# Token-major RWKV values for two groups at once, with put-off side steps and a longer recursion

## The chip, the cores and the metric

The kernel runs on one core of one Trainium2 chip. The metric is the device time of one execution in microseconds (us); lower is better. The engines are named as in the profile: PE is TensorE (PEld its weight loads), DVE is VectorE, ACT is ScalarE, POOL is GpSimd, SP is SyncE, which here only issues transfers.

## What is computed

One transformer block over 256 tokens of width 2048, in fp32: a normalised input is multiplied by one wide matrix `w_in`, three branches work on pieces of the product (attention, an RWKV-7 time mix, attention to a memory), and gated projections bring them back together. The change touches the RWKV branch:

```
proj = rms_norm(x, g) @ w_in                      # r_b, k_b, v_b, z_b: 1536 columns each
def token_shift_lerp(p, mu):
    prev = pad(p by one token)[:, :-1]
    return p + (prev - p) * mu                    # for r, k and v
# per head, over the tokens t:
sa    = state @ a_t
state = state * w_t + sa * b_t + v_t * k_t
y_t   = state @ r_t
# then a norm per head, plus sum(r*k*r_k) * v, times silu(z)
```

The scan is not run token by token. The kernel works on chunks of 128 tokens and solves a triangular system for each head and chunk.

## The kernel before

**Rounds.** The program is one list of jobs, each a slice of a weight matrix (`Job`). A job of 256 columns has four chunks of 512 KB and computes feature-major ("fm"): the weight slice is the stationary operand, the tokens stream, and for each of 16 row blocks and each half there is a matmul over 512 columns (L308) and one over 256 (L309), because each operand is split into a high and a low part. A "wide" job has 512 columns in eight chunks; there the tokens are stationary and three matmuls of 512 columns (L306) stand for each row block and half. One chunk is one round: 16 matmuls (8 pairs) of an fm job or 12 of a wide one. For each chunk SP issues one transfer (`issue_dma`, L259), ACT makes the high part (L270) and DVE the low part (L273). At most three chunks are loaded and three more split ahead.

**Side steps.** All else is written as Python generators ("lanes"). After each round `step_lanes` runs each lane that is due by one step, up to its next `yield`; `yield n` means n rounds of rest. `force` runs lanes with no round between. What a lane issues stands in every engine's queue right behind that round. Side results of PE go to the PSUM tile `psd`, of which there are four (`ps_side`); the rounds have four others (`pm`).

**RWKV.** Six groups of four heads (256 columns) each have jobs R, K, V and Z. `rkv_evac` and `shift_lerp` take a job's result: ACT copies two pieces per half, POOL adds (L323), POOL subtracts the shifted row (L435), DVE finishes (L431). `pairs_lane` makes decays (L521, L527, scans at L539) and the operands `AR` and `BK`; then, in one step, it transposes two arrays for head sums (L590) and V and BK to token-major `tok` (L599 to L601, read by ACT at L602 and DVE at L604). `rw_lane` makes Gram matrices (L622; DVE reads them at L626 and L627 with four `psd` tiles per chunk), inverts them in a recursion over 31 columns on DVE (L674, L678) that rests at each fourth column, joins blocks (L700 to L732), applies the inverse (L641, L743, L751 to L765), transposes back (L780), normalises, and transposes again (L817). `attn_a` is the attention of one group: scores L838 and L840, a softmax that ends with a scaling on ACT (L861), transposes L868, values L876 and L878, whose `psd` tile is read by L881 once `zsa` is there.

## Time and profile before

| what | value |
|---|---|
| median of 3 runs | 1479.6 us (1477.62 to 1480.51) |
| the profiled execution | 1478.29 us |
| its span, first to last instruction | 1476.5 us |
| PE busy | 1449.2 us, 98% of the span |
| DVE busy | 946.2 us, 64% |
| ACT busy | 747.3 us, 51% |
| POOL busy | 181.8 us, 12% |
| mean granted PE clock | 0.997 |

Busy time counts a matmul from its start to its modelled end, and matmuls overlap, so what one costs is read from start to start. Idle time of an engine stands in brackets behind the instruction that ended it. The RWKV and attention lanes lie in the first 735 us or so; afterwards come the memory branch and the projections.

### The profile page before, as it was taken

The page shows a single profiled execution, that of the slowest core. Times are in us where ns is not written, and L with a number is a line of the kernel's source. Part 1 is how long each engine was busy: PE and PEld are TensorE (multiplying, and loading weights), DVE is VectorE, ACT ScalarE, POOL GpSimd, SP SyncE. Part 2 cuts the span into 40 slices and gives each one's busy share as a digit, 9 for nine tenths or more (in the row PEclk, how much of TensorE's full clock was granted, in tenths as well). Part 3 has the DMA queues.
Part 4 walks back from the last instruction along what each step waited for, and adds up shares of the span by engine and source line. Part 5 has one row for each costly group of instructions (what it writes and reads, how often), then busy time and mean ns, then how long its engine had stood idle before and what let it go on. Part 6 is the DMA issues. An engine that isn't in the chain of part 4 may idle for free.

```text
span 1476.5 us, 22151 instructions
## 1 busy us (share of the span) xinstructions
PE 1449.2 (98%) x8315; PEld 1222.3 (83%) x8315; DVE 946.2 (64%) x1855; ACT 747.3 (51%) x1122; POOL 181.8 (12%) x252
## 2 busy tenths in 40 slices
PE   7999999999999999999999999999999999999997
PEld 6887888888888788788888888888888888888887
DVE  5778697796795786784666555655545545545555
ACT  5546546466456456445666454643443444444443
POOL 4312202212212222211100000000000000000011
PEclk9999999999999999999999999999999999999999
DMA  5665555456465465465575555566556556555753
GB/s 180 192 179 163 159 147 169 143 167 173 133 184 151 134 172 159 135 178 158 162 221 187 172 169 174 167 196 192 187 188 195 188 187 194 188 188 192 262 200 130
DMA packets 207968, 258.88 MB, mean 175 GB/s; under 512 B 28172, under 2 KB 146596, under 8 KB 207220
## 3 DMA queue, kind: packets, MB, share of 16 engines
q1 hardware_dynamic: 201872, 247.11, 54.5%
q10 hardware_dynamic: 4164, 6.71, 1.3%
q0 software_dynamic: 1824, 3.65, 0.8%
q8 instruction: 65, 1.06, 0.3%
q14 instruction: 43, 0.35, 0.1%
HBM read 253.74 MB, written 6.05 MB: 176 GB/s over the span
## 4 chain that ended last, share of the span: by engine, by line
PE 89%; DVE 4%; DMA 2%; ACT 1%; issue 1%; POOL 1%; SPq 0%; ACTq 0%; DVEq 0%
PE pm L306 43%; PE pm L308 24%; PE pm L309 12%; PE psd L622 2%; DVE wt L273 1%; DMA raw<-in_w_in_dram 1%; DVE fs_t L674 1%; PE psd L641 1%; PE psd L1037 1%; PE psd L743 1%; DMA NB<-d 1%; PE psd L154 1%; DMA x_sb<-in_x_dram 1%; ACT wt L270 1%; DVE X L678 1%
## 5 line engine op out<-in xcount | busy, mean ns | idle before, releaser
L273 DVE TENSOR_TENSOR wt<-raw,wt 128x1024 fp32r<-128x1024 f32 (+1 forms) x451 | 559.1, 1242 | 437.4 <-ACT wt L270 433.8
L270 ACT ACTIVATE wt<-raw 128x1024 fp32r<-128x1024 f32 (+1 forms) x452 | 477.2, 1057 | 494.0 <-PE pm L306 256.5
L308 PE MATMUL pm<-hT,wt 128*128 128x512 f32 (+1 forms) x1632 | 587.1, 402 | 0.0
L309 PE MATMUL pm<-hT,wt 128*128 128x256 f32 (+1 forms) x1632 | 458.5, 281 | 3.5 <-DVE wt L273 3.4
L308 PEld LDWEIGHTS pm<-hT,wt 128*128 128x128 f32 (+1 forms) x1632 | 305.7, 187 | 76.3 <-issue 4.2
L306 PE MATMUL pm<-wt,hT 128*128 128x512 f32 x1440 | 335.4, 391 | 0.0
L306 PEld LDWEIGHTS pm<-wt,hT 128*128 128x128 f32 x1440 | 268.6, 188 | 57.6 <-issue 1.7
L309 PEld LDWEIGHTS pm<-hT,wt 128*128 128x128 f32 (+1 forms) x1632 | 307.5, 188 | 6.2 <-DVE wt L273 6.0
L306 PE MATMUL pm<-wt,mg 128*128 128x512 f32 (+1 forms) x384 | 79.3, 367 | 0.0
L306 PEld LDWEIGHTS pm<-wt,mg 128*128 128x128 f32 x384 | 65.7, 189 | 12.5
L1183 POOL MEMSET sso<- 128x16 f32 x1 | 0.1, 117 | 607.0 <-PE pm L306 607.0
L674 DVE TENSOR_TENSOR fs_t<-X,NB 128x30 f32<-128x30 f32 (+13 forms) x354 | 64.9, 223 | 7.5 <-DMA NB<-d 7.1
L306 PE MATMUL pm<-wt,yas 128*128 128x512 f32 x288 | 67.6, 395 | 0.0
L306 PE MATMUL pm<-wt,ybs 128*128 128x512 f32 x288 | 67.6, 395 | 0.0
L323 POOL TENSOR_TENSOR lraw<-lraw,et 128x256 f32<-128x256 f32 (+1 forms) x38 | 45.1, 1207 | 167.2 <-ACT lraw L322 167.2
L306 PEld LDWEIGHTS pm<-wt,ybs 128*128 128x128 f32 x288 | 54.3, 188 | 12.6
L306 PEld LDWEIGHTS pm<-wt,yas 128*128 128x128 f32 x288 | 54.3, 188 | 12.7
L317 ACT ACTIVATE et<-pm 128x256 f32<-128x256 f32 (+1 forms) x112 | 42.6, 382 | 40.3 <-PE pm L309 37.6
L678 DVE TENSOR_TENSOR X<-X,fs_t 128x30 f32<-128x30 f32 (+13 forms) x354 | 56.3, 194 | 0.6
L306 PE MATMUL pm<-wt,mT 128*128 128x512 f32 x192 | 45.8, 395 | 0.0
L308 PE MATMUL pm<-mT,wt 128*128 128x512 f32 x128 | 45.4, 395 | 0.0
L306 PE MATMUL pm<-wt,ycs 128*128 128x512 f32 x192 | 45.3, 395 | 0.0
(299 smaller groups left out, 1324.3 us busy)
## 6 DMA issues: line engine op xcount, KB each, us to landing
raw<-in_w_in_dram SPq DMA_DIRECT2D x320, 512.0 KB, 3.7
raw<-in_w_mem_kv_dram SPq DMA_DIRECT2D x32, 512.0 KB, 3.5
raw<-in_w_out_dram SPq DMA_DIRECT2D x32, 512.0 KB, 4.4
raw<-in_w_proj_a_dram SPq DMA_DIRECT2D x24, 512.0 KB, 4.2
raw<-in_w_proj_b_dram SPq DMA_DIRECT2D x24, 512.0 KB
raw<-in_w_proj_c_dram SPq DMA_DIRECT2D x16, 512.0 KB, 4.4
NB<-d SPq DMA_DIRECT2D x24, 128.0 KB, 3.4
fr<-fd ACTq DMA_DIRECT2D x6, 385.0 KB
```

What stands on the lines that cost most here:

```text
L154: pe.transpose(pv[:, a, t], src[:, t, (k + a) * 128:(k + a + 1) * 128], ident)
L270: act.activation(w[:, :, 0], r, AF.Copy)
L273: eng.tensor_tensor(w[:, :, 1], r, w[:, :, 0].bitcast(FT), OP.subtract)
L306: pe.matmul(ps[:, 0:j.n], l, r, start=first and n == 0, stop=last and n == 2)
L308: pe.matmul(ps[0:j.m], hi, both, start=first, stop=last, skip_group_check=True)
L309: pe.matmul(ps[0:j.m, 256:512], lo, top, start=False, stop=last, skip_group_check=True)
L317: act.activation(t, ps[0:j.m, 256:512], AF.Copy)
L323: pool.tensor_tensor(j.dst[f], j.dst[f], t, OP.add)
L622: pe.matmul(pv[h][:, w].rearrange("p x t -> p (x t)"), BK[rows, q, c, w * 128:(w + 1) * 128], AR[rows, q, c].rearrange("p x t -> p (x t)") ...
L641: pe.matmul(pv[:, 2 * q + h], GS[:, c * 4 + 2 * q + h, 2], tok[:, q, c, rows], start=(c == 0), stop=True, skip_group_check=True)
L674: dve.tensor_tensor(t, X[:, k0:8, c:c + 1].to_broadcast([128, m, hi - lo]), NB[:, lo:hi, c].rearrange("p (o n) -> p o n", o=1).to_broadcas ...
L678: dve.tensor_tensor(X[:, k0:8, lo:hi], X[:, k0:8, lo:hi], t, OP.add)
```

## The change

Group V of two neighbouring groups becomes one wide job, so V comes token-major (`vt`) from PE, and needs no transposes. The shift by one token is now a shift across partitions: two transfers on SP copy `vt` to `vsh` one row down, POOL subtracts and multiplies by `mu_v` (which it loads as a row broadcast to 128 partitions), DVE adds (L507 of the new program). `tok` keeps only the two transposes of BK, in one `psd` tile. The Grams' readers of `tok` read `vt` instead. A lane may yield a pair: `(d, more)` rests d rounds, and then for up to `more` rounds goes on only if another lane has taken a `psd` tile in that round. `pairs_lane` no longer waits for V, and from the second group on it makes its transposes once the group before has finished its first half. The recursion rests at each third column. Jobs stand in another order. In the new program the recursion's L674 is L719, and the low part of the weights, L273, is L288.

```diff
+    used = [0]
     def ps_side():
+        used[0] += 1
         return psum.tile([128, 512], FT, name="psd", bufs=4)
...
     def step_lanes():
         clock[0] += 1
+        n = used[0]
+        due = [ln for ln in lanes if ln[0] <= clock[0]]
+        for ln in due:
+            if not ln[2]:
+                step(ln)
+        for ln in due:
+            if ln[2] and ln[0] <= clock[0]:
+                if used[0] != n or clock[0] >= ln[0] + ln[2]:
+                    ln[2] = 0
+                    step(ln)
...
+    def v_evac(g):
+        def f(ps, t):
+            if t == 0:
+                if g:
+                    force(("rw", g - 2))
+                for i in range(2):
+                    St["v", g + i] = E["rw"].tile([128, 2, 256], FT, name="vt", bufs=3)
+            for i in range(2):
+                act.activation(St["v", g + i][:, t], two(ps)[:, i], AF.Copy)
+            if t == 1:
+                add_lane(v_lane(g), 2)
+        return f
+    def v_lane(g0):
+        for g in (g0, g0 + 1):
+            vt = St["v", g]
+            sh = E["rw"].tile([128, 2, 256], FT, name="vsh")
+            mu = E["rw"].tile([128, 1, 256], FT, name="muv")
+            pool.memset(sh[0:1, 0], 0.0)
+            pool.dma_start(mu[:, 0], bass.AP(tensor=mu_v.tensor, offset=mu_v.offset + g * 256, ap=[[0, 128], [1, 256]]))
+            nc.sync.dma_start(sh[1:128], vt[0:127])
+            nc.sync.dma_start(sh[0:1, 1], vt[127:128, 0])
+            yield 3
+            pool.tensor_tensor(sh, sh, vt, OP.subtract)
+            pool.tensor_tensor(sh, sh, mu.to_broadcast([128, 2, 256]), OP.mult)
+            yield 2
+            dve.tensor_tensor(vt, vt, sh, OP.add)
+            flags["V", g] = True
+            yield 1
...
-        yield 3
+        yield (3, 2) if g else 3
...
-        yield from wait(("V", g))
-        yield 1
+        if g:
+            yield from wait(("half_free", g - 1))
...
-        v = St.pop(("V", g))
+        tok = rw.tile([128, 2, 2, 128], FT, name="tok")
+        p = ps_side()
+        pv = p.rearrange("p (a q c) -> p a q c", a=2, q=2)
+        for a in range(2):
+            for q in range(2):
+                pe.transpose(pv[:, a, q], BK[:, q, 0, 128 * (1 - a):128 * (2 - a)], ident)
+        act.activation(tok[:, :, 0], pv[:, 0], AF.Copy)
         for q in range(2):
-            p = ps_side()
-            pv = p.rearrange("p (a c) -> p a c", a=4)
-            for c in range(2):
-                pe.transpose(pv[:, c], v[:, q, c * 128:(c + 1) * 128], ident)
-            pe.transpose(pv[:, 2], BK[:, q, 0, 128:256], ident)
-            pe.transpose(pv[:, 3], BK[:, q, 0, 0:128], ident)
-            act.activation(tok[:, q, 0:3], pv[:, 0:3], AF.Copy)
...
-            if c % 4 == 0:
+            if c % 3 == 0 and c < 31:
                 yield 1
...
-        yield 3
+        yield (2, 2)
         pT = rw.tile([128, 2, 384], FT, name="pT")
...
-               Job(w_in2, VB + c, 256, 16, hT, rkv_evac(g, "V", "muv"), add=pool),
...
+    BJ = [Job(w_in2, VB + 512 * i, 512, 16, hT, v_evac(2 * i), mode="wide") for i in range(3)]
+    for g, (a0_, a1_) in enumerate(((0, 2), (2, 5), (5, 7), (7, 10), (10, 12), (12, 16))):
+        jobs += RJ[3 * g:3 * g + 2] + BJ[g // 2:g // 2 + 1 - g % 2] + AJ[a0_:a1_] + RJ[3 * g + 2:3 * g + 3 - (g == NG - 1)]
```

PE, the transposes of the second group. Before they share a round with the back transposes L780 of the group before and use five `psd` tiles:

```order
L306 MATMUL pm_1861<-wt_1807,hT_74 128x512 x6
L780 MATMUL psd_1919<-ident_85,YT_1707 128x128 x4
L590 MATMUL psd_1928<-ident_85,sg_1765 128x128 x4
L590 MATMUL psd_1934<-ident_85,R_1456 128x128 x4
L599 MATMUL psd_1942<-ident_85,V_1821 128x128 x2
L600 MATMUL psd_1942<-ident_85,BK_1845 128x128
L601 MATMUL psd_1942<-ident_85,BK_1845 128x128
L599 MATMUL psd_1950<-ident_85,V_1821 128x128 x2
L600 MATMUL psd_1950<-ident_85,BK_1845 128x128
L601 MATMUL psd_1950<-ident_85,BK_1845 128x128
```

Afterwards the same place on PE (L635 was L590, L645 was L600 and L601, L790 was L743, the product with the inverse):

```order
L321 MATMUL pm_1809<-wt_1667,hT_74 128x512 x6
L790 MATMUL psd_1816<-W_1784,XF_354 128x64 x4
L635 MATMUL psd_1822<-ident_85,sg_1702 128x128 x4
L635 MATMUL psd_1828<-ident_85,R_1403 128x128 x4
L645 MATMUL psd_1837<-ident_85,BK_1793 128x128 x4
L321 MATMUL pm_1802<-wt_1709,hT_74 128x512 x6
```

The transposes of V are gone, the others have moved up by three rounds to another neighbour, and the round uses four tiles. Next on PE, the first Gram chunk of that group, before in a round of its own:

```order
L306 MATMUL pm_1861<-wt_1849,hT_74 128x512 x6
L622 MATMUL psd_1977<-AR_1767,BK_1845 128x256
L622 MATMUL psd_1978<-AR_1767,BK_1845 128x256
L622 MATMUL psd_1977<-AR_1767,BK_1845 128x256
L622 MATMUL psd_1978<-AR_1767,BK_1845 128x256
L622 MATMUL psd_1987<-AR_1767,BK_1845 128x256
L622 MATMUL psd_1988<-AR_1767,BK_1845 128x256
```

Afterwards (L667 was L622, L812 was L765, the end of the second half of the group before):

```order
L810 MATMUL psd_1863<-GS_353,vt_835 64x128
L812 MATMUL psd_1863<-GS_353,W_1784 64x128
L667 MATMUL psd_1876<-AR_1704,BK_1793 128x256
L667 MATMUL psd_1877<-AR_1704,BK_1793 128x256
L667 MATMUL psd_1876<-AR_1704,BK_1793 128x256
L667 MATMUL psd_1877<-AR_1704,BK_1793 128x256
L667 MATMUL psd_1886<-AR_1704,BK_1793 128x256
L667 MATMUL psd_1887<-AR_1704,BK_1793 128x256
```

The Gram chunk has joined the round that ends the group before, and with that round's own tile it asks for five of the four. SP, from the Gram transfers of a group to those of its inverse, before:

```order
L259 DMA raw<-in_w_in_dram 128x2x512 x8
L259 DMA raw<-in_w_in_dram 128x4x256 x4
L652 DMA d_2057<-GS 32x8x32 x4
L259 DMA raw<-in_w_in_dram 128x4x256
L663 DMA NB<-d_2057 32x1024 x4
L259 DMA raw<-in_w_in_dram 128x4x256 x9
```

And afterwards (L697 was L652, L708 was L663, L274 is the weight transfer):

```order
L697 DMA d_3012<-GS 32x8x32 x4
L274 DMA raw<-in_w_in_dram 128x4x256
L708 DMA NB<-d_3012 32x1024 x4
L501 DMA vsh<-vt 127x512
L502 DMA vsh<-vt 1x16x16
L274 DMA raw<-in_w_in_dram 128x4x256 x6
L501 DMA vsh<-vt 127x512
L502 DMA vsh<-vt 1x16x16
L274 DMA raw<-in_w_in_dram 128x4x256 x6
```

The shifted copies of V stand between weight transfers, in the rounds of the recursion.

## Rows read from the trace of the kernel before

**Rows 1.** Stretch of the lanes: PE, PEld, DVE, ACT, POOL busy (instructions), clock, DMA share, GB/s.

```profile
100.00:700.00 600.00, 591.65 (x4080) 504.07 (x4079) 447.36 (x1259) 329.96 (x576) 127.75 (x178) 1.00 0.55 158
```

**Rows 2.** Waits of PE: us in total, times, longest.

```profile
PE pm L309 <- DVE wt L273: 3.4, 5, 0.9
PE psd L599 <- DVE Y L790: 3.4, 5, 0.9
```

**Rows 3.** Timeline of PE: start, us, what; fm pairs, then a wide job.

```profile
299.69 0.40 PE L308 MATMUL pm<-hT,wt 128*128 128x512 f32 x1
...
314.88 0.40 PE L308 MATMUL pm<-hT,wt 128*128 128x512 f32 x1
...
934.58 21.97 PE L306 MATMUL pm<-wt,hT 128*128 128x512 f32 x96
956.39 16.91 PE L306 MATMUL pm<-wt,yas 128*128 128x512 f32 x72
```

**Rows 4.** Timeline of PE: four transposes between rounds.

```profile
315.24 0.60 PE L817 MATMUL psd<-ident,Y 128*128 128x128 f32 x4
315.60 0.48 PE L308 MATMUL pm<-hT,wt 128*128 128x512 f32 x1
```

**Rows 5.** Timeline of PE: the transposes of groups 2 and 4, counted from 0.

```profile
284.25 0.60 PE L780 MATMUL psd<-ident,YT 128*128 128x128 f32 x4
...
287.04 0.48 PE L308 MATMUL pm<-hT,wt 128*128 128x512 f32 x1
...
492.74 0.60 PE L780 MATMUL psd<-ident,YT 128*128 128x128 f32 x4
...
495.15 0.41 PE L599 MATMUL psd<-ident,V 128*128 128x128 f32 x2 [0.93 <-DVE Y L790]
...
496.07 0.48 PE L308 MATMUL pm<-hT,wt 128*128 128x512 f32 x1
```

**Rows 6.** Timeline of PE: a Gram chunk of groups 0, 3 and 4.

```profile
80.42 2.78 PE L622 MATMUL psd<-AR,BK 64*128 64x256 f32 x16
...
394.57 2.00 PE L622 MATMUL psd<-AR,BK 64*128 64x256 f32 x16
...
499.02 1.56 PE L622 MATMUL psd<-AR,BK 64*128 64x256 f32 x10
501.15 1.10 PE L622 MATMUL psd<-AR,BK 64*128 64x256 f32 x6 [0.57 <-DVE GS L627]
```

**Rows 7.** Timeline of PE, then DVE: one attention tile, written and read.

```profile
426.96 0.38 PE L878 MATMUL psd<-pT,va 128*128 128x128 f32 x2
...
513.70 0.68 DVE L881 TENSOR_TENSOR ya<-psd,zsa 128x512 f32<-128x512 f32 x1
```

**Rows 8.** A stretch of group 0's recursion, columns as in the first group.

```profile
114.70:130.50 15.80, 13.55 (x73) 10.58 (x71) 14.35 (x72) 9.81 (x18) 2.66 (x5) 1.00 0.50 145
```

**Rows 9.** Timelines of DVE and of ACT in that stretch.

```profile
115.01 0.36 DVE L674 TENSOR_TENSOR fs_t<-X,NB 128x40 f32<-128x40 f32 x2
...
118.17 0.35 DVE L674 TENSOR_TENSOR fs_t<-X,NB 128x40 f32<-128x40 f32 x2
...
126.44 1.40 DVE L674 TENSOR_TENSOR fs_t<-X,NB 128x28 f32<-128x28 f32 x2
...
117.24 1.50 ACT L861 ACTIVATE as<-as,asm 128x256 f32<-128x256 f32 x4 [2.55 <-DVE asm L857]
...
120.58 2.94 ACT L270 ACTIVATE wt<-raw 128x1024 fp32r<-128x1024 f32 x3
```

**Rows 10.** Waits of DVE: us in total, times, longest.

```profile
DVE V L431 <- POOL et L435: 6.3, 6, 1.7
```

**Rows 11.** Groups by form: xcount | busy us, mean ns | idle before.

```profile
L273 DVE TENSOR_TENSOR wt<-raw,wt 128x1024 fp32r<-128x1024 f32 x448 | 556.3, 1244 | 437.4 <-ACT wt L270 433.8 <-PE pm L306 3.1
L435 POOL TENSOR_TENSOR et<-lraw 128x512 f32<-128x512 f32 x18 | 24.2, 1344 | 1.4
```

More of the change, by code (lines that the diff above doesn't have):

```diff
@@ L201, in add_lane @@
     def add_lane(gen, rest=0):
-        lanes.append([clock[0] + rest, gen])
+        lanes.append([clock[0] + rest, gen, 0])
     def later(rest, fn, *a):
@@ L208, in later, with step @@
         add_lane(g(), rest)
+    def step(ln):
+        try:
+            d = next(ln[1])
+            d, more = d if isinstance(d, tuple) else (d or 1, 0)
+            ln[0], ln[2] = clock[0] + d, more
+        except StopIteration:
+            lanes.remove(ln)
     def step_lanes():
         clock[0] += 1
-        for ln in list(lanes):
-            if ln[0] > clock[0]:
-                continue
-            try:
-                d = next(ln[1])
-                ln[0] = clock[0] + (d or 1)
-            except StopIteration:
-                lanes.remove(ln)
+        n = used[0]
[8 more added lines that the diff above has]
+                    step(ln)
     def force(*keys):
@@ L559, in pairs_lane @@
         AR = rw.tile([128, 2, 2, 2, 128], FT, name="AR", bufs=2)
-        tok = rw.tile([128, 2, 4, 128], FT, name="tok", bufs=2)
         nb = rw.tile([128, 2, 2, 2], FT, name="nb", bufs=2)
@@ L593, in pairs_lane @@
         dve.reciprocal(nb, nb)
[L594 to L605 removed]
+        tok = rw.tile([128, 2, 2, 128], FT, name="tok")
[5 more added lines that the diff above has]
+        act.activation(tok[:, :, 0], pv[:, 0], AF.Copy)
+        for q in range(2):
+            dve.tensor_tensor(tok[:, q, 1].rearrange("p (h v) -> p h v", h=2), pv[:, 1, q].rearrange("p (h v) -> p h v", h=2),
+                              nb[:, 0, q].rearrange("p (h o) -> p h o", o=1).to_broadcast([128, 2, 64]), OP.mult)
         flags["rkv_free", g] = True
@@ L612, in rw_lane @@
         S = E["S"]
+        vt = None
         halves = [slice(64 * h, 64 * h + 64) for h in range(2)]
@@ L640, in from_v @@
                 for h, rows in enumerate(halves):
-                    pe.matmul(pv[:, 2 * q + h], GS[:, c * 4 + 2 * q + h, 2], tok[:, q, c, rows], start=(c == 0), stop=True,
+                    pe.matmul(pv[:, 2 * q + h], GS[:, c * 4 + 2 * q + h, 2], vt[:, c, 128 * q + 64 * h:128 * q + 64 * h + 64], start=(c == 0), stop=True,
                               skip_group_check=True)
@@ L705, in rw_lane @@
             act.activation(X64[s, :, s], XN[s], AF.Copy)
+        yield from wait(("V", g))
+        vt = St["v", g]
         W = from_v(0)
@@ L750, in rw_lane @@
                     for h, rows in enumerate(halves):
-                        pe.matmul(pv[rows, q], tok[:, q, 2, rows], tok[:, q, 0, rows], start=True, stop=False)
-                        pe.matmul(pv[rows, q], tok[:, q, 3, rows], W[:, 1, q * 2 + h], start=False, stop=True)
+                        pe.matmul(pv[rows, q], tok[:, q, 0, rows], vt[:, 0, 128 * q + 64 * h:128 * q + 64 * h + 64], start=True, stop=False)
+                        pe.matmul(pv[rows, q], tok[:, q, 1, rows], W[:, 1, q * 2 + h], start=False, stop=True)
                 for rows in halves:
@@ L762, in rw_lane @@
                     u = c * 4 + 2 * q + h
-                    pe.matmul(pv[rows, q], tok[:, q, c, rows], GS[:, u, 3], start=(c == 0), stop=False,
+                    pe.matmul(pv[rows, q], vt[:, c, 128 * q + 64 * h:128 * q + 64 * h + 64], GS[:, u, 3], start=(c == 0), stop=False,
                               skip_group_check=True)
@@ L806, in rw_lane @@
                 Yq[:, c * 4:c * 4 + 4].rearrange("p (q h) v -> p q h v", q=2),
-                tok[:, :, c].rearrange("p q (h v) -> p q h v", h=2),
+                vt[:, c].rearrange("p (q h v) -> p q h v", q=2, h=2),
                 bs[:, c].rearrange("p q (h o) -> p q h o", o=1).to_broadcast([128, 2, 2, 64]), OP.mult)
@@ L812, in rw_lane @@
         yield from wait(("zsb", g))
+        yield (1, 2)
         p = ps_side()
```

9 lines of the change are left out of this document (2 added, 7 removed).

## The prediction

> **What bounds the kernel now.** I read the busy times by stretch first. Between 100 and 700 us, where the lanes run, PE is busy 591.65 of 600 us at a granted clock of 1.00, while DVE is busy 447.36, ACT 329.96 and POOL 127.75 [rows 1]. So TensorE is the bound; the time falls only if its queue gets shorter or one of its gaps closes. The waits of PE came second: what it waits for in the rounds is the split weights from DVE, 3.4 us in five waits, and in the transposes step a `psd` tile, 3.4 us in five waits, given free by a DVE operation of another lane [rows 2]. These are waits on the one late instruction; what the engine loses around them is larger, so I went through its timeline, from the start of one matmul to the start of the next.
>
> Three prices come from it. An fm pair (512 and 256 columns) takes 0.353 us: 43 pairs lie between 299.69 and 314.88. A wide job's matmul takes 0.227 us: 96 from 934.58 to 956.39 [rows 3]. Four transposes between two rounds hold the next main matmul back by 0.36 us, and that one takes 0.48 instead of the usual 0.40: 0.44 in all, 0.11 us for each instruction [rows 3, 4]. So a full-array side step pays for its instructions, and next to nothing for the interruption itself.
>
> **The change part by part.** *V as a wide job.* For two groups 2 x 4 chunks x 8 pairs = 64 pairs x 0.353 = 22.6 us become 8 chunks x 12 = 96 matmuls x 0.227 = 21.8: 0.8 us less, three times, -2.4 us, all on the path.
>
> Here a rule can be weighed against the trace. The trace has 0.353 us for 768 columns and 0.227 for 512 [rows 3]: per column the pair costs 4% more. The Trainium skill, TensorE: Matmul & The Clock Gate, section "Wait — 56ns, not 53.3ns?", gives a start to start of the columns at 2.4 GHz plus some 2.5 ns for each matmul. By that, as an estimate, a pair takes 0.325 us and a wide matmul 0.216, the three wide jobs save only 0.3 us, and the sum below comes out 2.1 us higher. The trace does not agree with it for either kind, so the sum goes by the rows.
>
> *Transposes.* 24 of V go (4 for each of six groups): 24 x 0.11 = -2.6 us. BK's stay. Both kinds of matmul that read `tok` keep their number and form.
>
> *Tiles in the transposes step.* Before, this step and the back transposes next to it take five tiles of four, 20 transposes. In group 2 they take 2.79 us, 284.25 to 287.04; in group 4 3.33, 492.74 to 496.07, with 0.93 of waiting [rows 5]. At 0.11 each, less what the last restart holds (counted above), 20 are 2.1 to 2.2. The excess in my walk through all six is 0.24 (group 0), about 0.68 (1 to 3) and 1.21 (4, 5): 4.7 us. Afterwards the round has four tiles (one of L790, two of L635, one of L645), so no tile has to come back within it. I take -4.7. Bounds: 0, if a tile is still held from the round before, to -4.7.
>
> *Grams.* A Gram chunk takes 2.00 us of PE in group 3, but 2.78 in group 0 and 3.23 (499.02 to 502.25) in group 4, where PE waits for DVE to empty the third pair [rows 6]. The reason in groups 4 and 5: an attention value tile is written at 426.96 and read only at 513.70, once `zsa` is there [rows 7], so three tiles are left for four. Four chunks x 1.23 + 0.78 = 5.7 us. The new job order makes that holding shorter: by the built program's order it falls on both chunks of group 4 and none of group 5, and group 0's chunk stays as it is. Left: 2 x 1.23 + 0.78 = 3.2, so -2.5. Bounds: 0 (group 5 is met too) to -5.7 (none is).
>
> *Put-off steps.* Interruptions of PE fall from 123 to 114. For full-array steps I cost a join at nothing, by the 0.11 that already holds the restart [rows 4]. A Gram chunk uses half of the rows (its form is 64 x 256 [rows 6]), and such steps show about 0.1 us more on entering or leaving; five of them now follow the likewise tiled end of the previous group's second half: -0.5. Against it: that round then asks for five tiles of four. The fourth Gram tile waits until ACT has copied the round's own first tile, while PE has the rest of that tile's and three Gram tiles' work before it, some 1 us; I take 0, and as the upper bound +1.23 a time, as where group 4 lacks a tile [rows 6]: +6.2 for five. Put-off steps (L868, L876, L817) issue no transfer of their own, so no queue is moved past. The Gram transfers come with their chunk, some three rounds earlier on SP; the `wd` and `wa` loads on POOL stay ahead of their lane's first rest.
>
> *Rests at three columns.* In group 0's recursion PE is busy 13.55 of 15.80 us and DVE 14.35 [rows 8]. One rest of four columns with its split takes 3.16 us (115.01 to 118.17) on DVE, and an fm round takes 8 x 0.353 = 2.83 on PE: DVE loses 0.3 us a round until the split weights run out. With the split at 1.24 [rows 11], a column is 0.48, and three with a split 2.7 us, under 2.83. A second cause stands beside it: ACT's L861 waits 2.55 us for a DVE operation behind the columns, and the splits on ACT start only at 120.58 [rows 9]. I take the gap of this stretch, 15.80 - 13.55 = -2.3 us; bounds 0 and -3.4, all of PE's waits for split weights [rows 2]. The later groups' recursions show little of it. Their longer recursion (two or three rounds more) delays only what follows in its lane, which is not last on PE.
>
> *New work.* The V lane puts two operations a group on POOL, six groups (twelve, some 1.34 us each by L435 [rows 11]), as V did before in three; their sum falls. They now stand in recursion rounds. DVE's add of V waits for POOL; behind it on DVE stand the splits, and behind those PE. Such a wait existed before: V's L431 waited for POOL 6 times, 6.3 us, the longest 1.7 [rows 10], and the chunks split ahead (three, 8.5 us of PE) hid it. On SP the copies of V wait for ACT's `vt` and POOL's memset, and weight transfers stand behind them; three loaded and three split chunks, 17 us, cover that. I take +1.0 for all this, with 0 to +18 (below), nearer to 0 because of that cover. A gain below 0 I exclude: it is added work, and DVE and POOL were not the bound.
>
> **Sum.** -2.4 - 2.6 - 4.7 - 2.5 - 0.5 - 2.3 + 1.0 = -14.0. The profiled execution has a span of 1476.5 and a time of 1478.29, so 1.8 lies outside; the median is 1.3 above it. 1476.5 - 14.0 + 1.8 = 1464.3, and + 1.3 = **1465.6 us**.
>
> **The rivals.**
> *Tile waits take the place of those removed.* The five joined Gram rounds have one tile too few. Each then costs what group 4's chunk costs, 1.23 [rows 6]: +6.2, 1471.8. For it: the tiles are exactly one short. Against: PE has about 1 us to do before the fourth, and only one ACT copy is needed.
>
> *The joins save more.* If rejoining side steps also spares the restart gaps that I put at zero, nine interruptions at 0.11 and the remaining Gram excess (3.2) go too: 1465.6 - 1.0 - 3.2 = 1461.4. Against it: the four-transpose step shows no such price [rows 4].
>
> *DVE and POOL hold each other up in the recursion.* One pair of L674 took 1.40 us at 126.44 where its like took 0.35 at 118.17 [rows 9]: 1.05 us lost while POOL was at work. Twelve POOL operations of V now stand there: 12.6 us on DVE. DVE has a quarter of its time free [rows 1], so I give half of it to PE, 6.3, and the gap of 2.3 stays: 1465.6 + 8.6 = 1474.2. If all of it reaches PE, 1480.5, no change. For it: POOL's work on V is moved to just where DVE was 91% busy [rows 8]. The Trainium skill, SBUF — State Buffer, section "Who interferes with whom", says that a DVE instruction with two SBUF inputs and a POOL instruction that reads SBUF exclude each other; L674 is such a one, and the row agrees.
>
> *Slower: the adds of V park DVE.* Each add (six) finds POOL still at its first operation and waits the longest wait seen plus one more operation, 1.7 + 1.34 = 3.0 us [rows 10, 11], and all reaches PE, since three columns and a split leave only 0.1 us a round to win the lead back: 6 x 3.0 = +18, 1483.6. It decides once the waits of one recursion together use up the three split chunks (8.5 us); with two V lanes in a row that takes other delays besides. Against it: the lane rests two rounds, 5.6 us, between POOL's operations (2.7) and the add.
>
> **How the numbers follow.** The measurement tells about 0.2%, 3 us, from no change. Chances: the forecast 0.52 (1465.6), tile waits 0.20 (1471.8), joins save more 0.08 (1461.4), half of the collisions 0.08 (1474.2), all of them 0.06 (1480.5, same), parked DVE 0.06 (1483.6, slower). Faster by over 0.2% is 0.52 + 0.20 + 0.08 + 0.08 = 0.88, within it 0.06, slower 0.06. The range must hold 0.8: from 1459, the larger gain with a little of the bounds of the Grams and the rests, to 1474, the tile waits with 2 us of unplanned gaps; the collisions and the parking are left out above.
>
> **What would show it.** In the profile after: the wide V jobs at 0.227 us a matmul; PE's count lower by 120; no wait of L635 or L645 for a tile; sixteen transposes in 1.8 us; the five joined Gram chunks (L667 behind L812) at 2.0 us, or at 3.2 if the first rival is right; PE's waits for split weights in group 0's recursion gone; L719 pairs of over 1 us few. Waits of DVE's L507 for POOL of over 3 us, followed by waits of PE for L288, would show the slower case. What would make the prediction wrong is a price for moved steps that the trace of before does not have: the same lanes now meet other neighbours in nearly every round, and a step that was covered may end last.

## The result: slower, by transfers that the sum had not priced

The changed kernel takes 1521.18 us (median of 4 runs, 1519.83 to 1523.54) against 1478.61 for the kernel before; the ratio is 1.0288, 95% interval 1.027 to 1.0307. It is 42.6 us slower where the prediction said 1465.6 and gave slower a chance of 0.06. The profiled execution has a span of 1519.0 us, against 1476.5.

The stretch of the lanes [rows 1], of the profile after (columns: length, then PE, PEld, DVE, ACT and POOL busy, granted clock, DMA share, GB/s), and PE's waits, which answer to [rows 2]:

```profile
100.00:700.00 600.00, 558.23 (x3661) 471.08 (x3659) 422.50 (x1202) 299.68 (x511) 122.91 (x176) 0.96 0.53 151
```

```profile
PE pm L323 <- ACT wt L285: 31.0, 6, 11.1
PE pm L324 <- DVE wt L288: 7.9, 13, 1.0
```

PE is idle 41.8 of 600 us where it was idle 8.4, and what it waits for is new: the high part of the weights, made by ACT (L285, which was L270), 31.0 us in six waits, one of them 11.1 long. The waits of the transposes for a tile are gone.

To see which steps held, I added up PE's timeline of each kernel from start to start in three parts: the main matmuls at their undisturbed price, the side steps with what entering and leaving them costs, and the gaps between main matmuls. How the parts are parted moves each by a us or two; the differences between kernels depend on it less.

| kernel | main, us | side steps, us (interruptions) | gaps, us |
|---|---|---|---|
| before | 1269.5 | 187.7 (123) | 4.7 |
| changed | 1267.3 | 177.1 (113) | 59.8 |

Main matmuls and side steps fell by 12.8 us, against 2.4 + 2.6 + 4.7 + 2.5 + 0.5 = 12.7 in the prediction. The gaps grew by 55.1, where the prediction had -2.3 + 1.0. So the change does to PE's queue what it was costed at, and the miss is in the gaps.

Where they begin is in SP's timeline (start, us, engine, line) and in PE's:

```profile
91.08 0.78 SPq L501 DMA_DIRECT2D vsh<-vt  x1
91.91 4.30 SPq L502 DMA_DIRECT2D vsh<-vt  x1
96.25 19.59 SPq L274 DMA_DIRECT2D raw<-in_w_in_dram  x6
115.97 0.70 SPq L501 DMA_DIRECT2D vsh<-vt  x1
116.72 6.93 SPq L502 DMA_DIRECT2D vsh<-vt  x1
```

```profile
103.93 0.28 PE L324 MATMUL pm<-hT,wt 128*128 128x256 f32 x1
108.13 0.80 PE L323 MATMUL pm<-hT,wt 128*128 128x512 f32 x1 [3.92 <-ACT wt L285]
...
110.17 0.63 PE L323 MATMUL pm<-hT,wt 128*128 128x512 f32 x1
110.61 0.41 PE L324 MATMUL pm<-hT,wt 128*128 128x256 f32 x1
110.82 0.63 PE L323 MATMUL pm<-hT,wt 128*128 128x512 f32 x1
...
129.47 0.28 PE L324 MATMUL pm<-hT,wt 128*128 128x256 f32 x1
140.88 0.79 PE L323 MATMUL pm<-hT,wt 128*128 128x512 f32 x1 [11.14 <-ACT wt L285]
```

Behind each copy of V (L501) weights are issued, and PE then runs dry. POOL's first use of the first two copies, and ACT's split of the first weight chunk behind the first copy, show what they waited for:

```profile
106.06 1.26 POOL L504 TENSOR_TENSOR vsh<-vsh,vt 128x512 f32<-128x512 f32 x1 [8.82 <-DMA vsh<-vt]
...
136.56 1.26 POOL L504 TENSOR_TENSOR vsh<-vsh,vt 128x512 f32<-128x512 f32 x1 [19.31 <-DMA vsh<-vt]
```

```profile
107.02 1.06 ACT L285 ACTIVATE wt<-raw 128x1024 fp32r<-128x1024 f32 x1 [10.59 <-DMA raw<-in_w_in_dram]
```

The trace also holds when the parts of a transfer report that they are done; I call these marks, and the last mark is the landing. By them the six copies of 254 KB land 14.4 to 20.3 us after their issue. The six weight chunks of 512 KB issued behind the first two copies land after 10.7 to 16.1 us, where the median over the run is 3.7. A weight chunk has 16 marks; a copy has two, one about 1 us after its issue and one at its end. Of the chunk issued at 96.25, fifteen marks are there by 100.15 and the last comes at 106.94, just behind the copy, which lands at 105.70. So one sixteenth of the chunk waits behind the copy, and the chunk is complete only with it. Except in the third of these stretches the DMA engines are almost idle:

```profile
94.00:96.00 2.00, 2.00 (x13) 1.72 (x13) 2.00 (x9) 0.90 (x4) 0.77 (x1) 1.00 0.05 16
106.00:108.00 2.00, 0.00 (x0) 0.00 (x0) 0.00 (x0) 0.98 (x1) 1.86 (x2) 0.59 0.07 22
110.00:112.00 2.00, 2.00 (x7) 1.71 (x8) 2.00 (x11) 1.01 (x1) 0.00 (x0) 0.50 0.91 257
138.00:140.00 2.00, 0.00 (x0) 0.00 (x0) 0.00 (x0) 0.23 (x1) 1.16 (x1) 0.50 0.07 24
```

The last two columns are the share of the 16 DMA engines and GB/s. They are 0.05 and 16 GB/s while the copy is all that moves (first row), 0.07 and 22 to 24 GB/s while little more than what is left of the weight chunks behind a copy moves (second and fourth), and 0.91 with 257 GB/s once that is through. One of sixteen engines is 0.0625. The clock column tells a second part of the price: around these two idle stretches PE's clock fell to 0.50, that is 1.2 GHz, and a pair takes 0.65 us (110.17 to 110.82) instead of 0.353 [rows 3].

### The profile page after: what moved, and what is told of

Its sections match the earlier page's. It is cut to its first block, busy times and chain, and to the rows that moved or that the text cites. A ratio compares the mean times of both kernels' runs of the same rounds, so it can differ in the third digit from the quotient of the medians.

```text
span 1519.0 us, 21882 instructions
## 1 busy us (share of the span) xinstructions
PE 1457.3 (96%) x8195; PEld 1222.7 (80%) x8195; DVE 938.9 (62%) x1837; ACT 740.1 (49%) x1103; POOL 171.0 (11%) x251
## 3 DMA queue, kind: packets, MB, share of 16 engines
q8 instruction: 64, 1.05, 0.3%
## 4 chain that ended last, share of the span: by engine, by line
PE 79%; DMA 8%; DVE 7%; ACT 2%; issue 1%; SPq 1%; POOL 0%; ACTq 0%; DVEq 0%
PE pm L321 43%; PE pm L323 17%; PE pm L324 9%; DMA raw<-in_w_in_dram 6%; DVE wt L288 3%; PE psd L667 1%; ACT wt L285 1%; DVE fs_t L719 1%; DMA fr<-fd 1%; DVE X L723 1%; PE psd L686 1%; PE psd L1085 1%; PE psd L790 1%; DMA x_sb<-in_x_dram 1%; PE psd L157 1%
## 5 line engine op out<-in xcount | busy, mean ns | idle before, releaser
L288 DVE TENSOR_TENSOR wt<-raw,wt 128x1024 fp32r<-128x1024 f32 (+1 forms) x451 | 557.6, 1238 | 477.5 <-ACT wt L285 473.9
L285 ACT ACTIVATE wt<-raw 128x1024 fp32r<-128x1024 f32 (+1 forms) x452 | 476.5, 1056 | 538.0 <-PE pm L321 274.0
L323 PE MATMUL pm<-hT,wt 128*128 128x512 f32 (+1 forms) x1440 | 527.9, 408 | 31.0 <-ACT wt L285 31.0
L324 PE MATMUL pm<-hT,wt 128*128 128x256 f32 (+1 forms) x1440 | 410.4, 285 | 7.9 <-DVE wt L288 7.9
L321 PE MATMUL pm<-wt,hT 128*128 128x512 f32 x1728 | 408.0, 393 | 2.2 <-ACT wt L285 1.5
L321 PEld LDWEIGHTS pm<-wt,hT 128*128 128x128 f32 x1728 | 322.2, 188 | 73.1 <-issue 3.2
L323 PEld LDWEIGHTS pm<-hT,wt 128*128 128x128 f32 (+1 forms) x1440 | 275.2, 191 | 100.4 <-ACT wt L285 33.1
L324 PEld LDWEIGHTS pm<-hT,wt 128*128 128x128 f32 (+1 forms) x1440 | 276.4, 192 | 13.5 <-DVE wt L288 13.2
L719 DVE TENSOR_TENSOR fs_t<-X,NB 128x30 f32<-128x30 f32 (+13 forms) x354 | 64.7, 222 | 9.8 <-DMA NB<-d 9.6
L321 PEld LDWEIGHTS pm<-wt,yas 128*128 128x128 f32 x288 | 54.3, 188 | 12.6
L321 PEld LDWEIGHTS pm<-wt,ybs 128*128 128x128 f32 x288 | 54.3, 188 | 12.6
L332 ACT ACTIVATE et<-pm 128x256 f32<-128x256 f32 (+1 forms) x100 | 38.0, 382 | 37.0 <-PE pm L324 35.3
L321 PEld LDWEIGHTS pm<-wt,ycs 128*128 128x128 f32 x192 | 36.2, 188 | 8.4
```

Of the source, the lines that this page charges most:

```text
L285: act.activation(w[:, :, 0], r, AF.Copy)
L288: eng.tensor_tensor(w[:, :, 1], r, w[:, :, 0].bitcast(FT), OP.subtract)
L321: pe.matmul(ps[:, 0:j.n], l, r, start=first and n == 0, stop=last and n == 2)
L323: pe.matmul(ps[0:j.m], hi, both, start=first, stop=last, skip_group_check=True)
L324: pe.matmul(ps[0:j.m, 256:512], lo, top, start=False, stop=last, skip_group_check=True)
L332: act.activation(t, ps[0:j.m, 256:512], AF.Copy)
```

## The experiments

**One engine, or something else about the copies.** Theory: the copy of 127 rows lies on one DMA engine, and weights, which need all sixteen, wait behind it there. The first run cuts the copy:

```diff
-            nc.sync.dma_start(sh[1:128], vt[0:127])
+            nc.sync.dma_start(sh[1:113], vt[0:112])
+            nc.sync.dma_start(sh[113:128], vt[112:127])
```

> The changed kernel with each shifted copy of V (127 rows of 2 KB) issued as two transfers, one of 112 rows and one of 15; nothing else differs. Theory (the copy of 127 rows runs on one of the sixteen DMA engines, since 127 has no divisor up to 16, and weight chunks, which need all sixteen, wait behind it): both transfers land in a few us instead of 14, PE's waits for ACT's and DVE's weight splits (31.0 and 7.9 us) all but vanish, and the time falls from 1521 to about 1466 (1463 to 1472). Rival 1 (a copy from SBUF to SBUF is slow whatever its shape): no change, 1515 to 1525. Rival 2 (the copies park SP until POOL's memset and ACT's evacuation are done, and the weights behind them come late): no change, 1515 to 1525.

Measured 1481.65 us, ratio to before 1.0015 (1.0005 to 1.0024). By the marks the pieces land 3.7 to 7.3 us after their issue, PE's wait for ACT's L285 in fm rounds falls from 31.0 to 0.5 us, and 39.5 us are back. That leaves the theory standing and the first two rivals down; but the time is 16 us above what was expected.

```diff
-            pool.memset(sh[0:1, 0], 0.0)
...
-            nc.sync.dma_start(sh[1:128], vt[0:127])
+            pool.memset(sh, 0.0)
```

> The changed kernel without the copy of the 127 rows (the shifted V is left at zero but for one row, so V's values differ); the one-row transfer stays. It is the ceiling for any mending of that copy. Theory: within 0.2% of the split copy, about 1465. Rival 1: far below the split copy (some 55 us). Rival 2 (SP parked): the one-row copy still waits for ACT and POOL, so the time stays above 1500.

1482.21 us, ratio 1.0022 (1.0012 to 1.0032). The copy is left out, so V's shift is too: without it the kernel is no better than with it cut, so the cut copy costs nothing that can be measured, and the missing 16 us lie elsewhere. The expected time was missed for that reason.

```diff
-            nc.sync.dma_start(sh[1:128], vt[0:127])
+            nc.scalar.dma_start(sh[1:128], vt[0:127])
```

> The changed kernel with the 127-row copy issued on ACT's queue instead of SP's, shape unchanged. Theory (one DMA engine is the bottleneck): the copy still takes 10 us or more and slows the weights that pass that engine, but they are no longer strictly behind it: 1470 to 1505, between the split copy and the changed kernel. Rival 2 (SP's order alone): as good as the split copy, about 1466.

1514.81 us, ratio 1.0243 (1.0223 to 1.0264), 10 us above the expected range. PE waits 23.8 us for DVE's splits and 8.9 for ACT's. The other queue gives back 6.4 of the 39.5 us, so SP's order is not the main thing. The marks show why: the copies land after 17.4 to 21.0 us here, and of a weight chunk issued on SP beside one, at 87.75, fifteen marks are there by 91.85 and the last at 100.79.

```diff
-            nc.sync.dma_start(sh[0:1, 1], vt[127:128, 0])
+            pool.memset(sh[0:1, 1], 0.0)
```

> The changed kernel without the one-row copy between the two token halves (one row of the shifted V is zero); the 127-row copy stays. SP spends 4 to 7 us on that one-row issue. Theory: that time is only the queue being full behind the large copy, so the time stays at 1515 to 1522. Rival 3 (the one-row copy, cut into sixteen pieces of 64 bytes, is what blocks SP): 1480 or less.

1523.37 us, ratio 1.0301 (1.0281 to 1.0322), with one row of the shift left out. The one-row copy is not the cause, though SP spends 4.3 to 6.9 us on it.

A later run asked which row counts are slow, with the cut at another place:

```diff
-            nc.sync.dma_start(sh[1:113], vt[0:112])
-            nc.sync.dma_start(sh[113:128], vt[112:127])
+            nc.sync.dma_start(sh[1:127], vt[0:126])
+            nc.sync.dma_start(sh[127:128], vt[126:127])
```

> The split-copy kernel with the cut at another place: 126 rows in one transfer and the last row in another. 126 is 14 x 9, not a multiple of 16. Theory in its form so far (rows are dealt in equal shares to the largest number of engines, up to sixteen, that divides them): fourteen engines take nine rows each, the copy lands in a few us, 1479 to 1485. Rival (only row counts that are a multiple of 16 are spread, all others run on one engine; the 15 rows of the split copy were too small to show it): the copy takes some 14 us, 1515 to 1525.

1480.33 us, ratio 1.0014 (1.0004 to 1.0024), the copies of 126 rows landing after 3.7 to 5.8 us. 126 rows are as good as 112 and 15, and 127 take 14.4 us or more. A copy of 112 rows has 16 marks, one of 126 rows 15, one of 127 rows two. The Trainium skill, DMA: Bandwidth & Descriptors, section "Why a DMA increments its semaphore by 16 and not by 1", states the rule: a copy from SP or ACT goes to the largest number of engines, sixteen at most, that divides the slowest dimension, and it names 127 partitions as a case of one. These runs agree: 126 has the divisor 14, and 16, 14 and one late marks fit sixteen engines, fourteen and one, with one early mark where not all sixteen take part.

**Where the other 16 us are.** In the split-copy kernel PE's gaps are 18.2 us against 4.7, and most of them stand in the recursions of groups 0, 2 and 4, the groups in whose recursion the V lane runs (group 3 has one too, see below). One stretch of it, and DVE's and POOL's timelines in there:

```profile
300.00:325.00 25.00, 22.78 (x127) 19.13 (x126) 24.86 (x88) 11.67 (x25) 8.88 (x9) 1.00 0.60 167
```

```profile
305.88 1.36 DVE L720 TENSOR_TENSOR fs_t<-X,NB 128x15 f32<-128x15 f32 x2
307.18 1.35 DVE L724 TENSOR_TENSOR X<-X,fs_t 128x15 f32<-128x15 f32 x2
308.46 0.30 DVE L720 TENSOR_TENSOR fs_t<-X,NB 128x14 f32<-128x14 f32 x2
...
305.64 1.47 POOL L505 TENSOR_TENSOR vsh<-vsh,vt 128x512 f32<-128x512 f32 x1
307.19 1.32 POOL L506 TENSOR_TENSOR vsh<-vsh,muv 128x512 f32<-128x512 f32 x1
```

DVE is busy 24.86 of 25 us, and PE stands still for 2.2. The two operations of the V lane on POOL (L505, L506) hold up one pair of the recursion's operations each: 1.36 and 1.35 us instead of 0.30. Summed over all six recursions, what L720 and L724 (L674 and L678 before) take above the median of their shape is 13.1 us before and 26.9 here. The next four runs go from the split-copy kernel. The first leaves the V lane's arithmetic out:

```diff
-            pool.tensor_tensor(sh, sh, vt, OP.subtract)
-            pool.tensor_tensor(sh, sh, mu.to_broadcast([128, 2, 256]), OP.mult)
...
-            dve.tensor_tensor(vt, vt, sh, OP.add)
```

> The split-copy kernel without the arithmetic of the V lane (POOL's subtraction and product and DVE's sum are left out, so V is not shifted); the transfers and the order of all else stay. It asks what that arithmetic costs in the recursion rounds, where PE lost 13 us more to DVE's splits than before. Theory (POOL's operations lock out DVE's, and with the added sum make DVE late in the recursions of groups 0, 2 and 4): the excess of L720 and L724 over their usual time falls from 26.9 to about 14 us, PE's gaps go by 9 to 13 us, time 1469 to 1473. Rival (the recursion rounds are late because of the steps of the group before, its norm, that now stand in them): 1477 to 1481.

1470.05 us, ratio 0.9935 (0.992 to 0.995): 11.6 us less. The excess is 15.1 us, the gaps 9.2. So the V lane's arithmetic is most of the rest, and the steps of the group before are not.

```diff
-            pool.tensor_tensor(sh, sh, vt, OP.subtract)
-            pool.tensor_tensor(sh, sh, mu.to_broadcast([128, 2, 256]), OP.mult)
+            dve.tensor_tensor(sh, sh, vt, OP.subtract)
+            dve.tensor_tensor(sh, sh, mu.to_broadcast([128, 2, 256]), OP.mult)
```

> The split-copy kernel with the V lane's subtraction and product on DVE instead of POOL (12 operations, by the sum's 0.69 us 8.3 us more on DVE), in the same rounds. Theory (a POOL operation of 1.3 us takes more from DVE than the same operation costs DVE itself): DVE's lockouts fall by about 13 us for 8.3 us of work, time 1475 to 1481, not above the split copy. Rival (DVE's own load makes it late, POOL's help is free): 1487 to 1492.

1478.48 us, ratio 0.9993 (0.9984 to 1.0002): 3.2 us less than with POOL's help. The excess is 15.6 us. The three runs fit one price, as an estimate. On DVE the lane takes 18 operations of 0.69, 12.4 us, and costs 8.4 us more than no lane; with POOL it takes 4.1 us of sums and 11.8 of lockout, 15.9, and costs 11.6. So in these rounds PE loses about 0.7 us for each us taken from DVE.

```diff
-            if c % 3 == 0 and c < 31:
+            if c % 2 == 0:
```

> The split-copy kernel with the recursion resting at each second column, sixteen rests of two columns. DVE then has per round 1.24 + 2 x 0.48 = 2.2 us of fixed work against 2.83 of PE. Theory (DVE's load per round is what starves PE): most of the 13 us of added gaps go, 1468 to 1473. Rival (a few long lockouts and waits, not the load, make the gaps): 1478 to 1483. If the longer recursion delays the end of a lane that something waits for, a new wait shows there.

1498.84 us, ratio 1.0131 (1.0114 to 1.0147): the expected gain is there and something else is lost. The gaps fall from 18.2 to 8.7 us, as the theory has it, but the side steps rise from 177.3 to 208.4:

```profile
PE psd L866 <- DVE fs_t L720: 15.7, 4, 7.3
PE psd L866 <- DVE Y L858: 9.9, 1, 9.9
```

L866 (L817 before) is the pair of transposes at the end of a group's lane. With five rests more (fifteen for ten) the lane is not done when the next Z job's result needs its buffers, `force` runs the rest of it with no round between, and PE waits out each step. The groups follow each other every 28 rounds, and the lane has no five to spare.

```diff
-        jobs += RJ[3 * g:3 * g + 2] + BJ[g // 2:g // 2 + 1 - g % 2] + AJ[a0_:a1_] + RJ[3 * g + 2:3 * g + 3 - (g == NG - 1)]
+        jobs += BJ[g // 2:g // 2 + 1 - g % 2] + RJ[3 * g:3 * g + 2] + AJ[a0_:a1_] + RJ[3 * g + 2:3 * g + 3 - (g == NG - 1)]
```

> The split-copy kernel with each wide V job ahead of R and K of its first group instead of behind them, so that the V lane's copies, POOL operations and sums fall before that group's recursion, into rounds where DVE has time. Theory (the V lane in the recursion rounds makes DVE late): as without the arithmetic, 1468 to 1474. Rival (steps of the group before do): 1477 to 1482.

1537.49 us, ratio 1.0386 (1.037 to 1.0403). Here too lanes are forced: side steps 225.1 us, PE's L866 waits 15.7 and 9.0 us for DVE. So the run tells nothing of the V lane's place.

**Putting the lane off.** From the split-copy kernel, the first of the two V lanes waits ten rounds more:

```diff
-            yield 3
+            yield 13 if g == g0 else 3
```

> The split-copy kernel with the first V lane's POOL and DVE operations put off by ten rounds, so that they fall behind that group's recursion and ahead of the first reader of V, and the second's into the rounds after; all the work of the reference is done. Theory (the V lane's operations inside the recursion rounds cost PE 11 to 12 us, the same operations outside cost next to nothing): 1470 to 1474, 0.4 to 0.7% under the kernel before. Rival (the work costs the same wherever it stands, since DVE is short in all rounds of the lanes): 1478 to 1482.

1478.61 us, ratio 0.9999 (0.9989 to 1.0008). That is the rival's number, but not for the rival's reason: in the profiled execution, a slower one of 1482.09 us, the gaps are 21.1 us and the largest stand at the ends of the same recursions, and the excess is 24.2. DVE and POOL at the end of group 2's recursion:

```profile
335.36 2.31 DVE L720 TENSOR_TENSOR fs_t<-X,NB 128x14 f32<-128x14 f32 x2
337.59 0.29 DVE L724 TENSOR_TENSOR X<-X,fs_t 128x14 f32<-128x14 f32 x2
337.80 1.26 DVE L720 TENSOR_TENSOR fs_t<-X,NB 128x24 f32<-128x24 f32 x1
...
336.33 1.30 POOL L505 TENSOR_TENSOR vsh<-vsh,vt 128x512 f32<-128x512 f32 x1
337.71 1.30 POOL L506 TENSOR_TENSOR vsh<-vsh,muv 128x512 f32<-128x512 f32 x1
```

In the program L505 stands behind the recursion. On the chip it runs at 336.33, while DVE is still in the last columns, which end at 341. POOL waits for its own operands alone, so a place in the order doesn't hold it, and the lockouts come along.

```diff
-        yield 2
+        yield 3
...
-            if c % 3 == 0 and c < 31:
+            if c % 3 == 1 and 1 < c < 31:
```

> As the put-off V lane, and the recursion starts one round later behind the transfers of its operand and rests at nine columns instead of ten, so it ends in the same round. DVE waited 9.6 us in five places for these transfers at the head of a recursion, and in group 3 weight chunks came late behind that. Theory (that wait makes the gap of 3 to 4 us in group 3): 1467 to 1471, below the kernel with the put-off V lane alone. Rival (DVE has the lead to bear the wait, and four columns at once make it late): same or 1 to 3 us more.

1478.17 us, ratio 0.9997 (0.9989 to 1.0006): the same. The rival's case. DVE's waits for the operand's transfers are gone (10.3 us in the run before), and group 3's gap stays (it begins at 416 us), so they were not its cause.

```diff
-        yield (2, 2)
+        yield 3
...
-        yield (1, 2)
```

> The put-off V lane with the plain rests of the kernel before in place of the rests that wait for another interruption (all four places undone). Theory of the prediction (joining full-array steps saves nothing, the joined Gram chunks 0.5 us and do so through the earlier transposes, not through these rests): within 2 us of the put-off V lane. Rival (each interruption spared saves a restart): 3 to 5 us more. Lanes end up to three rounds earlier, which may move the gaps of the recursions either way.

1478.47 us, ratio 1.0002 (0.9992 to 1.0012), inside the interval of the put-off lane, as the prediction's theory has it. The same pair on a kernel without the lockouts is the last run below.

**A transfer that weights wait for.** In group 3 of the split-copy kernel SP waits 10.9 us for the attention's bias rows, 385 KB that ACT issues at 399.83, and PE's gap follows. First SP's waits (us in total, times, longest), then the timelines:

```profile
SPq L274 <- DMA fr<-fd: 14.7, 2, 10.9
```

```profile
400.95 0.39 SPq L274 DMA_DIRECT2D raw<-in_w_in_dram  x1
...
414.59 6.49 SPq L274 DMA_DIRECT2D raw<-in_w_in_dram  x4
...
418.37 1.06 ACT L285 ACTIVATE wt<-raw 128x1024 fp32r<-128x1024 f32 x1 [7.03 <-DMA raw<-in_w_in_dram]
...
419.48 0.49 PE L321 MATMUL pm<-wt,hT 128*128 128x512 f32 x1 [1.41 <-ACT wt L285]
```

By the marks the bias rows land at 414.52, and the chunk issued at 414.59, which reports to the same semaphore, follows at once. So this wait makes group 3's gap. The bias rows take 14.7 us, as I read it, for the reason that the copies did: their outermost dimension is 2, and they have three marks, one early and two late. The first edit moves them to SP:

```diff
-        nc.scalar.dma_start(fr[2 * g:2 * g + 2],
+        nc.sync.dma_start(fr[2 * g:2 * g + 2],
```

> The split-copy kernel with the attention's bias rows (L436, fr from fd) issued by SP instead of ACT. SP waited 14.7 us in two places for a transfer that ACT had not yet issued or just had, because weight transfers wait for the earlier transfer that uses the same completion semaphore; in group 3 the weights came late behind that and PE lost some 4 us at 418 us. Theory (that wait is the cause of group 3's gap): the gap at 418 goes, SP's wait for fr falls under 1 us, 1476 to 1479. Rival (group 3's gap comes from DVE's load like the others): the gap stays, 1481 to 1483.

1490.32 us, ratio 1.0072 (1.006 to 1.0084): SP's wait for them is gone, and the time is 8.7 us longer, with new gaps (near 56, 61, 140 and 670 us) that start as this one does:

```profile
56.92 0.50 PE L321 MATMUL pm<-wt,hT 128*128 128x512 f32 x1 [0.92 <-ACT wt L285]
58.18 3.39 PE L321 MATMUL pm<-wt,hT 128*128 128x512 f32 x12 [0.76 <-DVE wt L288]
```

The bias rows still take 12.4 to 13.0 us, and now the weights stand behind them: near five of the six, chunks land after 7.4 to 13.0 us instead of 3.8. Theory and rival both missed this.

The following two go from the put-off lane with nine rests and have that edit in them as well. The first:

```diff
-            pool.tensor_tensor(sh, sh, vt, OP.subtract)
-            pool.tensor_tensor(sh, sh, mu.to_broadcast([128, 2, 256]), OP.mult)
+            dve.tensor_tensor(sh, sh, vt, OP.subtract)
+            dve.tensor_tensor(sh, sh, mu.to_broadcast([128, 2, 256]), OP.mult)
```

> The put-off V lane with its three operations all on DVE, the recursion one round later with nine rests, and the bias rows on SP. Put off by rounds alone, POOL still ran its two operations early, in the last rounds of the recursion (336.33 and 337.71 us against the recursion's end at 341.0), because POOL's queue is ahead of DVE's; on DVE they stand where they are written. Theory (POOL's operations lock DVE out in the recursions of groups 0, 2 and 4): the excess of L720 and L724 falls from 6.6, 5.6 and 5.0 us to 2 to 4 in each, PE's gaps of 1.8 to 2.8 us at the end of those recursions go, 1466 to 1472. Rival (these gaps come with any work there): 1476 to 1480.

1479.65 us, ratio 0.9994 (0.9983 to 1.0004). The lockouts are gone (14.4 us in all), the gaps at the ends of the recursions too; the time is the rival's, and the bias rows on SP were a possible reason. The second leaves the two operations on POOL, later:

```diff
-            yield 13 if g == g0 else 3
+            yield 15 if g == g0 else 3
...
-            yield 2
+            yield 1 if g == g0 else 2
             dve.tensor_tensor(vt, vt, sh, OP.add)
```

> As the run with all on DVE, but with the V lane's two operations on POOL, two rounds later still in the order of the program, directly ahead of the sum. Theory: POOL now meets the blocks after the recursion, with few DVE operations to lock out: 1465 to 1472. Rival (POOL is further ahead of DVE than two rounds): the lockouts in the last columns stay, 1474 to 1478.

1492.57 us, ratio 1.0086 (1.0073 to 1.0099). The excess is down to 13.9 as well, so POOL did meet other work. But the sum now stands directly ahead of V's first reader, and PE waits for it: 6.7 us at L687, and side steps of 191.5 us.

Then the lane late and on DVE (the first of these two) with the bias rows on ACT's queue, as in the changed kernel:

```diff
-        nc.sync.dma_start(fr[2 * g:2 * g + 2],
+        nc.scalar.dma_start(fr[2 * g:2 * g + 2],
```

> The put-off V lane with its three operations on DVE and the recursion at nine rests, but the bias rows on ACT's queue again, as in the changed kernel: the run before it differs from this one in that queue alone. With the bias rows on SP the split-copy kernel lost 8.7 us and PE had new gaps at 56, 61, 140 and 670 us where that transfer went ahead of weights. Theory (POOL's lockouts made the gaps at the recursions' ends, and they are cured here; the bias rows on SP hid it): 1479.7 - 8.7 = 1471, 1468 to 1474. Rival (the rest of the 14 us lies elsewhere): 1477 to 1480.

**1469.95 us, ratio 0.9933 (0.992 to 0.9945)**: 9.9 us under the kernel before, as expected. DVE at the end of group 2's recursion, and the stretch of the lanes:

```profile
333.47 0.26 DVE L720 TENSOR_TENSOR fs_t<-X,NB 128x14 f32<-128x14 f32 x2
...
335.01 0.18 DVE L720 TENSOR_TENSOR fs_t<-X,NB 128x24 f32<-128x24 f32 x1
...
337.29 0.69 DVE L505 TENSOR_TENSOR vsh<-vsh,vt 128x512 f32<-128x512 f32 x1
338.01 0.69 DVE L506 TENSOR_TENSOR vsh<-vsh,muv 128x512 f32<-128x512 f32 x1
```

```profile
100.00:700.00 600.00, 593.21 (x4052) 504.90 (x4052) 455.24 (x1243) 327.04 (x566) 113.73 (x170) 1.00 0.59 163
```

The last columns take 0.26 and 0.18 us where they took 2.31 and 1.26, the lane's operations follow behind, and PE is busy 593.21 of 600 us. The kernel with the lockouts left in (1478.17) and this one differ in the engine of twelve operations alone: 8.2 us (9.5 by the two ratios), for an excess of 22.1 against 14.3. Neither edit does it by itself: against the split copy, DVE in the old place gave 3.2 us and POOL in the new one 3.0, both together 11.7. The time is that of the kernel without the arithmetic (1470.05).

With the bias rows on POOL's queue instead:

```diff
-        nc.scalar.dma_start(fr[2 * g:2 * g + 2],
+        pool.dma_start(fr[2 * g:2 * g + 2],
```

> The same with the bias rows on POOL's queue, whose transfers have completion semaphores of their own. Theory (in group 3 weight transfers wait for the bias rows' semaphore, 10.8 us on SP, and PE loses some 4 us at 416 us): that gap goes, 2 to 4 us less than with ACT's queue, 1465 to 1470. Rival (the transfer itself is in the way of the weights, whichever queue it is on): same or more, 1471 to 1480.

1480.7 us, ratio 1.0004 (0.9995 to 1.0013): the rival's case. SP's wait is gone and group 3's gap falls from 2.9 to 1.1 us, but the weight chunks that overlap the bias rows land after 7.3 us (median) here, 7.2 with the rows on SP (the lane late on DVE) and 5.6 with them on ACT, against 3.8 elsewhere. Why ACT's queue does least harm stays open, and no run gave the bias rows a shape for more than two engines.

Last, that version with the plain rests (all four places):

```diff
-        yield (3, 2) if g else 3
+        yield 3
...
-        yield (2, 2)
+        yield 3
```

> The best version so far (split copy, V's arithmetic late and on DVE, nine rests) with the plain rests of the kernel before instead of those that join another interruption. Theory of the prediction (a join of full-array steps saves only its restart, 0.1 us, and seven interruptions are at stake): 0 to 3 us slower, 1470 to 1473. Rival (joins are worth more, tile waits come back without them): 4 us or more, 1474 to 1478.

1468.41 us, ratio 0.9927 (0.9914 to 0.9941), not to be told from 1469.95. Side steps are 179.3 us in 120 interruptions against 177.6 in 113. The rests that wait for company earn nothing that can be measured.

## Why the prediction was wrong, step by step

- **V as a wide job** held: main matmuls are 2.2 us shorter (predicted 2.4).
- **Transposes and their tiles** held. The step of group 4, to be set against [rows 5]:

```profile
517.26 1.00 PE L790 MATMUL psd<-W,XF 128*128 128x64 f32 x8
518.10 0.61 PE L635 MATMUL psd<-ident,sg 128*128 128x128 f32 x4
518.54 0.60 PE L635 MATMUL psd<-ident,R 128*128 128x128 f32 x4
518.98 0.60 PE L645 MATMUL psd<-ident,BK 128*128 128x128 f32 x4
519.33 2.98 PE L321 MATMUL pm<-wt,hT 128*128 128x512 f32 x12
```

  Twenty instructions in 2.07 us, 0.10 each, and no wait; it was 3.33. (I had counted sixteen here; L790 has eight.)
- **Grams** held: group 4's two chunks still pay 1.23, group 5's no longer, as read from the program's order. Group 0's 0.78 went as well, but its transposes now wait 1.4 us for DVE's BK.
- **The first rival, tile waits in the five joined rounds,** did not come. Twenty tiled matmuls and sixteen of the Gram chunk together take 3.85 us, the sum of the two alone; the one at 522.15 takes 1.23 more because group 4 lacks a tile anyway. That a join of full-array steps is worth nothing held too.
- **Rests at three columns** brought no gain in the changed kernel: the columns per round fell, but the lane's arithmetic filled DVE again (24.86 of 25 us with the split copy). With the lane late on DVE (1469.95) the step held: PE's three waits for splits in group 0's recursion (0.76, 0.54 and 0.86 us before) are gone, and its gaps there fall from 2.7 to 0.7 us, against the -2.3 of the sum.
- **New work** is the step that failed. Its words were "On SP the copies of V wait for ACT's `vt` and POOL's memset, and weight transfers stand behind them; three loaded and three split chunks, 17 us, cover that." I priced the wait for the copies' operands, and took their own time, which I never priced, for that of any transfer. They land after 14.4 to 20.3 us and keep the weights behind them 10.7 to 16.1, and two come within 25 us, more than the cover bears: 39.5 us by the split copy. The bound of +18 was one of POOL and DVE, and no term had the landing in it.
- **The rival of DVE and POOL** (0.08 for half, 0.06 for all, 6.3 or 12.6 us) was right in mechanism and place: twelve operations, each holding up a pair by 1.05 us, 12.6 us, where the runs show 11.8 of lockout, and 11.6 us of time for lockouts and sums together. I gave it too little, because I counted DVE as a quarter free over the whole stretch [rows 1], when in those rounds it was nearly full [rows 8].
- **Parked sums** did not come: behind the late copies DVE's splits wait for ACT, not for V's sum.

With both failed terms mended the kernel takes 1468 to 1470 us, 3 to 4 above the forecast. Group 3's gap, 2.9 us in the run of 1469.95, is most of that; it was not there before, and the prediction had no term for the bias rows.

## What to carry to other kernels

A transfer has two prices, the wait before it is issued and its own time, and the second depends on its shape: a copy one partition down has 127 rows, a prime number, and runs on one DMA engine; cut it into 112 and 15, or 126 and 1. Where a transfer lands late, look at its outermost dimension; here a 2 made 385 KB take 12 us and more. Before moving POOL work next to DVE work with two operands in SBUF, read how busy DVE is in those very rounds, not over the program; and to put such work off, tie it to DVE (or do it there), since rounds of rest don't hold POOL. A lane that has no round to spare turns each further rest into a forced stop.

## What the runs showed of the hardware that I had not expected

- One slow transfer holds up all that share its DMA engine: weight chunks behind a copy of 127 rows landed after 10.7 to 16.1 us instead of 3.7, with fifteen of sixteen marks there some 7 us earlier for the chunk of 96.25, and with the copy on ACT's queue they still took up to 13.0 us (1514.81 us).
- A POOL operation of 1.3 us cost DVE about as much as the operation takes (0.30 became 1.36 us), so twelve of them were dearer than doing the work on DVE at 0.69 us each.
- Around idle stretches of 4 to 11 us PE's granted clock fell to 0.50 and a pair took 0.65 us instead of 0.353, so a gap costs more than its length.
- The same 385 KB, two by 128 rows, land only after 12.3 us or more on any queue, and cost 8.7 to 9.7 us more on SP's queue and 10.8 us more on POOL's than on ACT's (1490.32 against 1481.65, 1479.65 against 1469.95, 1480.7 against 1469.95).
